# Router scores and choice per chunk of 128 tokens, and the shared expert's down products moved behind unit 9

## The chip, the core and the metric

The program runs on one core of a Trainium2 chip. The core has five engines with queues of their own: PE (TensorE, matrix products), DVE (VectorE), ACT (ScalarE), POOL (GpSimd) and SP (SyncE, which here does nothing but issue DMAs). Each queue is worked off in order; engines wait for each other through semaphores. The metric is the device time of one execution in microseconds (us).

## The reference

Two transformer blocks over 256 tokens of width 1024, one after the other. The first has a pooling mixer, an attention layer and two dense feed-forward layers. The second has a gated recurrent mixer and then a mixture of experts. Only the last part matters here, cut to this:

```
h   = rms_norm(x, g_pre_ffn) * (1 + sc2) + sh2            # 256 x 1024
s   = sigmoid(h @ w_router); sel = s + b_router           # 64 experts
# 8 groups of 8 experts; a group's score is the sum of its two best sel
# keep the 4 best groups, then the 8 best experts of those
w   = s[top8] / sum(s[top8]) * 2.5
y   = sum over the 8 experts e of w_e * swiglu(h, w_gu[e], w_down[e])
y  += swiglu(h, w_sh_gu, w_sh_down)                       # the shared expert
out = x + gt2 * rms_norm(y, g_post_ffn)
```

An expert has a 1024 x 512 gate-up matrix and a 256 x 1024 down matrix, 3 MB in float32. All 64 experts are read, 192 MB.

## The kernel before

All of it is one straight program; its author writes the order of each engine's instructions by hand. The 256 tokens are two chunks (c = 0, 1) of 128, one token per partition.

**Up to the router.** `post` ends the mixer: it forms the residual x (`resid`), the normed input of the experts (`second`, in the tile `yg`), turns it by PE transposes into `h2T` (`flip`, `copies`), and splits `yg` into a high and a low part in `h2` (`parts`: a cast on ACT, a subtraction on POOL). Then come the router's scores (one product for all 256 tokens, L1512, a sigmoid, two transposes back, L1518) and, in `route`, the choice on DVE for both chunks at once, which ends in the mask `M` of chosen experts, the weights `W`, and, through three small products with triangular and all-one matrices (L1557 to L1559), each token's rank within its expert (`slot1`).

**The shared expert's gate-up product** needs 16 float32 products of 128 x 128 by 512 (L1585). They are a generator, and `fill(n)` puts the next n of them into PE's queue, between the router's steps: `GU_AT` says how many at four places, and `route` issues what is left behind the rank products. Its down products (L1610, four groups, one for each chunk and half of the output) start the four PSUM accumulators `acc`, and stand inside unit 0: `first_fill` puts two groups where later units add the unit before them, and two follow with `self.down(1, 0)` and `self.down(1, 1)`.

**The units.** The 64 experts are worked off in 28 units, `UNITS = "FFFFSSMHMSMMHMSMMHMSMMMHSMMM"`: F and M hold two experts with room for 64 tokens each, S four with 32, H one with 128. For every second unit PE gathers the tokens of two units (L1792). Then each unit has a gate-up product `front` (L1809), the silu on ACT and its product on DVE (L1814), and `back`: transposes (L1824, L1829), the down product (L1841), and split results that the next unit adds into `acc` (L1853). `sides()` hides the placement of experts into units behind units 0 to 4; from unit 4 on the expert to load is read from its result, `plan`.

**The loads.** Expert weights come as tiles of 128 x 2048 floats (1 MB), three for each expert (two gate-up, one down), issued on SP's queue in the order of use (L1735) into 17 slots: 11 of the tag `ex` in the pool `ep`, and 6 in `ep2`, which opens when the dense weights are gone. A slot is taken again in the order in which its users end in the program. At the start `yg` holds one of the 11 slots, the shared expert's weights three (`wsh`, L1746), and seven take expert tiles. So 3 + 7 + 6 loads go ahead of the router, and the next ones wait in turn for `yg`, the two gate-up tiles of `wsh`, the six tiles of unit 0, the down tile of `wsh`, the tiles of unit 1, and so on. From the 25th expert tile on, a tile takes the slot of the tile 17 places before it. `self.loads(...)` only puts issues into SP's queue; when they start is decided by the slots.

One more transfer: the row `GP2`, 1024 gains spread over 128 partitions (512 KB, POOL's queue, L173), needed only at the end, is read behind unit 0's front.

Of the kernel before, what the change touches and what calls it, by code (L numbers as in the profile page):

```python
# [22 lines left out]
TAIL = 2  # L23
# [66 lines left out]
GU_AT = (4, 1, 1, 6)  # L90
# [58 lines left out]
class Kern:  # L149
# [936 lines left out]
    def mixer(self):  # L1086
# [320 lines left out]
    def post(self, ctx, ws_ctx):  # L1407
# [17 lines left out]
        lg = tmp[0:64, 128:384]  # L1425
# [13 lines left out]
        def resid(c, h, r, eng):  # L1439
            sl = hs[h]  # L1440
            V.scalar_tensor_tensor(x[:, c, sl], yg[:, c, sl], r, x[:, c, sl], op0=ALU.mult, op1=ALU.add)
            eng.tensor_tensor(yg[:, c, sl], x[:, c, sl], G2[:, sl], op=ALU.mult)

# [44 lines left out]
        resid(1, 0, r, nc.gpsimd)  # L1488
        resid(1, 1, r, nc.gpsimd)
# [4 lines left out]
        self.loads(3 + NEX - 4 + NEX2)  # L1494
        flip(0)
# [20 lines left out]
        self.pl = self.pst([128, 2, 64])  # L1516
        for c in range(2):
            nc.tensor.transpose(self.pl[:, c, :], lg[:, 128 * c:128 * c + 128], self.ident[0:64, 0:64])  # L1518
        self.dump("xl2", x)


    def route(self):

        nc, A = self.nc, self.A
        tmp = _Arena(self.small([128, 1024], "grow", 3))
        t3 = lambda tag, shape=(128, 2, 64): tmp.tile(list(shape))
        br, tri8, pl = self.br, self.tri8, self.pl
        self.fill(GU_AT[3])
        sel = t3("sel")
        nc.vector.tensor_tensor(sel, pl, br[:, None, :].to_broadcast([128, 2, 64]), op=ALU.add)  # L1530

        m8 = t3("m8", (128, 16, 8))
        sg = sel.rearrange("p c (g e) -> p (c g) e", e=8)
        for i in range(16):
            nc.vector.max(m8[:, i, :], sg[:, i, :])
        gs = t3("gs", (128, 2, 8))
        nc.vector.tensor_tensor(gs.rearrange("p c g -> p (c g)"), m8[:, :, 0], m8[:, :, 1], op=ALU.add)
        g8, gn = t3("g8", (128, 2, 8)), t3("gn", (128, 2, 8))
        for c in range(2):
            nc.vector.max(g8[:, c, :], gs[:, c, :])  # L1540
        nc.vector.memset(g8[:, :, 4:8], -3.0e38)
        for c in range(2):
            nc.vector.match_replace(gn[:, c, :], g8[:, c, :], gs[:, c, :], -3.0e38)
        nc.vector.tensor_tensor(gn, gn, gs, op=ALU.is_equal)
        nc.vector.copy_predicated(sg, gn.rearrange("p c g -> p (c g)")[:, :, None].to_broadcast([128, 16, 8]).bitcast(I32),
# [3 lines left out]
        for c in range(2):  # L1549
            nc.vector.max(top[:, c, :], sel[:, c, :])  # L1550
# [193 lines left out]
    def tiles(self):  # L1744
# [3 lines left out]
        for n in range(NUNIT):  # L1748
            yield from self.load_unit(n)
# [346 lines left out]
```

## Time and profile before

| | |
|---|---|
| three timed runs | 1332.06, 1332.54, 1334.05 us; median 1332.54 us |
| the profiled execution | 1334.75 us, of which the span from first to last instruction is 1332.9 us (1.85 us lie around it) |
| busy share of the span | PE 96%, PE weight loads 69%, DVE 48%, ACT 39%, POOL 17% |
| moved by DMA | 374.45 MB; the slices from 933 us to 1300 us show 405 to 421 GB/s each, the mean of the span is 281 GB/s |
| granted PE clock, mean | 0.988 of full speed |

The dense part fills the span up to about 830 us, the router lies between 830 and 853 us, and the 28 units follow up to 1323 us. An engine's busy time counts its instructions from start to end. A timeline's row gives the start, the length, the engine, the line of the kernel, the operation, what is written and read (a tile's name without its number), the shape and how many instructions were merged; in brackets stands how long the engine sat idle before it and what ended that. A float32 product counts as two PE instructions. The granted clock 1.00 is the level of 2.4 GHz, 0.50 that of 1.2 GHz.

### The profile page before, as it was taken

Reading aid. Unit: us, or ns where it says so; the run is one execution under the profiler, and the core shown is the slowest. Engines: PE = TensorE matmul, PEld = TensorE weight load, DVE = VectorE, ACT = ScalarE, POOL = GpSimd, SP = SyncE. Lnnn points to the kernel's source line nnn. Section 1 sums busy time; section 2 is a strip of 40 time slices with the busy share of each in tenths; the row PEclk is TensorE's granted clock in tenths of the full one; section 3 lists DMA queues with packets and bytes.
Section 4 is the critical chain, followed back from the end, with each engine's and each line's share of the span. In section 5 each row is a group of like instructions: output and inputs, shape, how many; then the busy total and the mean of one; then the engine's idle time right before and its main releaser. Section 6 shows DMA issues by size and latency. Waiting matters only on the chain. (4 is left out here: it accounts for less than half of the span.)

```text
span 1332.9 us, 20200 instructions
## 1 busy us (share of the span) xinstructions
PE 1274.2 (96%) x7812; PEld 922.1 (69%) x7812; DVE 646.2 (48%) x984; ACT 526.0 (39%) x883; POOL 228.3 (17%) x230
## 2 busy tenths in 40 slices
PE   7999999999999999989988899999998999999986
PEld 5889887988798998878887897544453443534532
DVE  5664555846657456576879557423222222222223
ACT  6534444557554456556645345311111111111112
POOL 1111112123033000125246442200000000000000
PEclk8999999999999999999999999999999999999998
DMA  8768678444485575646434478799999999999994
GB/s 301 252 231 280 248 270 316 155 164 159 130 326 189 189 249 194 221 151 242 143 104 136 152 274 342 273 372 378 405 420 420 419 420 419 420 419 420 421 420 192
DMA packets 72817, 374.45 MB, mean 281 GB/s; under 512 B 8932, under 2 KB 9364, under 8 KB 44304
## 3 DMA queue, kind: packets, MB, share of 16 engines
q1 hardware_dynamic: 68912, 361.25, 71.3%
q0 software_dynamic: 3664, 11.89, 2.8%
q8 instruction: 62, 1.02, 0.3%
q14 instruction: 35, 0.29, 0.1%
q10 hardware_dynamic: 144, 0.01, 0.0%
HBM read 371.99 MB, written 1.11 MB: 280 GB/s over the span
## 5 line engine op out<-in xcount | busy, mean ns | idle before, releaser
L137 DVE TENSOR_TENSOR wlo<-wland,whi 128x1024 fp32r<-128x1024 f32 x201 | 244.2, 1249 | 104.4 <-ACT whi L134 103.6
L258 PE MATMUL pw<-hT,whi 128*128 128x256 f32 x1856 | 250.6, 282 | 0.0
L134 ACT CAST whi<-wland 128x1024 fp32r<-128x1024 f32 x236 | 237.2, 1046 | 25.2 <-PE pa L267 12.7
L258 PEld LDWEIGHTS pw<-hT,whi 128*128 128x128 f32 x1856 | 232.9, 189 | 12.6 <-ACT whi L134 6.5
L1809 PE MATMUL pw<-ex,xg 128*64 128x512 f32 (+2 forms) x1024 | 208.5, 596 | 5.0 <-DMA ex<-ex 4.8
L1809 PEld LDWEIGHTS pw<-ex,xg 128*64 128x64 f32 (+2 forms) x1024 | 65.7, 130 | 133.3 <-issue 107.4
L258 PE MATMUL pw<-hT,wlo 128*128 128x256 f32 x928 | 128.2, 280 | 0.0
L1841 PE MATMUL pw<-ex,al 128*64 128x512 f32 (+2 forms) x512 | 113.2, 613 | 7.9 <-DMA ex<-ex 7.9
L258 PEld LDWEIGHTS pw<-hT,wlo 128*128 128x128 f32 x928 | 117.2, 189 | 0.2 <-POOL wlo L137 0.2
L137 POOL TENSOR_TENSOR wlo<-wland,whi 128x1024 fp32r<-128x1024 f32 x35 | 87.4, 2497 | 162.7 <-ACT whi L134 127.9
L267 PE MATMUL pa<-whi,hT 128*128 128x512 f32 x352 | 114.6, 401 | 0.0
L1814 DVE TENSOR_TENSOR a<-sil,pw 128x256 f32<-128x256 f32 x28 | 11.8, 421 | 190.5 <-ACT sil L1812 190.5
L1846 DVE SCALAR_TENSOR_TENSOR grow<-pw,sw,yh 128x512 fp32r<-128x512 f32 x56 | 42.1, 751 | 111.9 <-ACT yh L1845 111.0
L1812 ACT ACTIVATE sil<-pw 128x256 f32<-128x256 f32 x28 | 10.8, 385 | 209.0 <-PE pw L1809 209.0
L700 POOL TENSOR_TENSOR al<-a,ah 128x256 fp32r<-128x256 f32 x44 | 32.6, 742 | 326.9 <-ACT ah L699 326.9
L1841 PEld LDWEIGHTS pw<-ex,al 128*64 128x64 f32 (+2 forms) x512 | 31.9, 132 | 74.9 <-issue 49.9
L1845 ACT ACTIVATE yh<-pw,sw 128x512 fp32r<-128x512 f32 x56 | 38.5, 688 | 111.1 <-PE pw L1841 111.1
L694 ACT ACTIVATE sil<-pw 128x256 f32<-128x256 f32 x44 | 16.9, 384 | 164.7 <-PE pw L258 164.7
L1780 POOL TENSOR_TENSOR grow<-hx,Wp 128x256 f32<-128x256 f32 x24 | 14.7, 630 | 383.7 <-DVE hx L1778 383.7
L267 PEld LDWEIGHTS pa<-whi,hT 128*128 128x128 f32 x352 | 66.5, 189 | 16.1 <-DVE hT L248 0.4
L267 PE MATMUL pa<-wlo,hT 128*128 128x512 f32 x176 | 70.2, 399 | 5.0 <-DVE wlo L137 3.4
L267 PE MATMUL pa<-wlo,ah 128*128 128x512 f32 x176 | 69.8, 397 | 0.5 <-DVE wlo L137 0.5
(400 smaller groups left out, 1780.8 us busy)
## 6 DMA issues: line engine op xcount, KB each, us to landing
ex<-ex SPq DMA_DIRECT2D x192, 1024.0 KB
wland<-wd SPq DMA_DIRECT2D x236, 512.0 KB
ada<-ada SPq DMA_DIRECT2D x24, 1024.0 KB
row<-rows POOLq DMA_DIRECT2D x6, 512.0 KB, 4.9
ex<-exs SPq DMA_DIRECT2D x3, 1024.0 KB
bias<-bscr POOLq DMA_DIRECT2D x4, 512.0 KB, 4.8
x<-x SPq DMA_DIRECT2D x4, 256.0 KB
pw<-poolw SPq DMA_DIRECT2D x2, 512.0 KB
```

Source lines behind the costliest of these rows:

```text
L134: nc.scalar.copy(h, t)
L137: eng.tensor_tensor(l, t, h, op=ALU.subtract)
L258: self.nc.tensor.matmul(out, a[:, o:o + 128], b[:, k, :], start=(p == 0 and k == 0), stop=(p == 2 and k == nk - 1))
L267: self.nc.tensor.matmul(out, a[:, k, cs], b[:, lo:lo + n], start=(first and p == 0), stop=(last and p == 2))
L694: nc.scalar.activation(sil, ps[:, 0:256], AF.Silu)
L700: nc.gpsimd.tensor_tensor(al[:, 0, :], a, ah[:, 0, :], op=ALU.subtract)
L1780: nc.gpsimd.tensor_tensor(view(ow), view(oh), W[:, :, :, None].to_broadcast(shape), op=ALU.mult)
L1809: nc.tensor.matmul(gu[r * e:r * e + r, :], xg[:, k, o + r * e:o + r * e + r], w[k // 4][:, 512 * (k % 4):512 * (k % 4) + 512], start=(k == ...
L1814: nc.vector.tensor_tensor(act, sil, gu[:, 256:512], op=ALU.mult)
L1841: nc.tensor.matmul(y[r * e:r * e + r, :], aT[:, f, r * e:r * e + r], w[2][:, 1024 * f + 512 * nb:1024 * f + 512 * nb + 512], start=(f == 0 ...
L1845: nc.scalar.activation(yh[:, sl], y, AF.Copy, scale=sw)
L1846: nc.vector.scalar_tensor_tensor(yl[:, sl], y, sw, yh[:, sl], op0=ALU.mult, op1=ALU.subtract)
```

## The change

The scores are computed with the tokens on the partitions at once: per chunk eight products with 64 columns (`logits`), a sigmoid (`scores`), and the choice on DVE (`choose`, for one chunk). Chunk 0's choice is put ahead of chunk 1's scores in the program. All of `yg`'s gains for chunk 1 go to DVE (POOL before). Seven shared gate-up products now stand ahead of the rank products and nine behind (twelve and four before; the last number of `GU_AT` is not used any more). The shared expert's down products go behind unit 9 (`DOWN_AT`): unit 0 then starts the accumulators, the down weights are loaded behind unit 8's tiles into an ordinary slot, an eighth expert tile takes their old slot at the start, and the load of `GP2` stands behind the down products.

```diff
-GU_AT = (4, 1, 1, 6)
+GU_AT = (4, 1, 2, 2)
+DOWN_AT = 9
...
-                self.ex, self.nload, self.nex = {}, 0, 4
+                self.ex, self.nload, self.nex = {}, 0, 3
                 self.yg = self.tile8([128, 2, 1024])
-                self.wsh = [self.tile8([128, 2048]) for _ in range(3)]
+                self.wsh = [self.tile8([128, 2048]) for _ in range(2)]
...
+        acc = [first(1, 0)]
         r0 = self.rstd(sx[0], 1024)
-        acc = [first(1, nb) for nb in range(2)]
+        acc.append(first(1, 1))
...
-        resid(1, 0, r, nc.gpsimd)
-        resid(1, 1, r, nc.gpsimd)
+        for h in range(2):
+            sums(1, h, r)
+        for h in range(2):
+            gains(1, h, V)
...
+        def logits(c):
+            for k in range(8):
+                nc.tensor.matmul(pl[:, c, :], h2T[:, k, 128 * c:128 * c + 128], wrt[:, k, :], start=(k == 0), stop=(k == 7))
+
+        def scores(c):
+            nc.scalar.activation(lg[:, c, :], pl[:, c, :], AF.Sigmoid)
+
         flip(0)
         copies(0, nc.scalar.copy, nc.scalar.copy)
+        logits(0)
         sqx(1, 0)
         sqx(1, 1)
         r1 = self.rstd(sx[1], 1024)
         self.warm(AF.Sigmoid)
+        scores(0)
         self.shared = self.shared_products()
         self.fill(GU_AT[0])
         for h in range(2):
             second(1, h, r1)
         flip(1)
-        copies(1, nc.scalar.copy, V.tensor_copy)
+        copies(1, nc.scalar.copy, nc.scalar.copy)
+        choose = self.choices()
+        choose(0)
+        self.fill(GU_AT[1])
+        logits(1)
         parts(0)
+        scores(1)
+        self.warm(AF.Silu)
         parts(1)
-        self.fill(GU_AT[1])
-        pg = self.pst([64, 256])
-        for k in range(8):
-            nc.tensor.matmul(pg, wrt[:, k, :], h2T[:, k, :], start=(k == 0), stop=(k == 7))
-        nc.scalar.activation(lg, pg, AF.Sigmoid)
-        self.warm(AF.Silu)
+        choose(1)
         self.fill(GU_AT[2])
...
+        def go(c):
+            V.tensor_tensor(sel[:, c, :], lg[:, c, :], br, op=ALU.add)
+
+            sg = sel[:, c, :].rearrange("p (g e) -> p g e", e=8)
+            for i in range(8):
+                V.max(m8[:, c, i, :], sg[:, i, :])
+            V.tensor_tensor(gs[:, c, :], m8[:, c, :, 0], m8[:, c, :, 1], op=ALU.add)
...
+            V.copy_predicated(sg, gn[:, c, :, None].to_broadcast([128, 8, 8]).bitcast(I32),
+                              self.low[:, :, None].to_broadcast([128, 8, 8]))
...
+            V.tensor_tensor(M[:, c, :], rep[:, c, :], sel[:, c, :], op=ALU.not_equal)
...
         for i in range(3):
+            if i == 2:
+                for n in range(DOWN_AT):
+                    yield from self.load_unit(n)
+                self.wsh.append(self.tile_ex())
             self.nc.sync.dma_start(out=self.wsh[i], in_=self.A["exs"][:, 2048 * i:2048 * i + 2048])
             yield 1
-        for n in range(NUNIT):
+        for n in range(DOWN_AT, NUNIT):
             yield from self.load_unit(n)
...
-            if n == 0:
-                GP2 = self.row(self.rows, 7 * 1024, 1024)
-                pend = first_fill
...
             if n == 0:
-                self.down(1, 0)
                 next(side)
-                self.down(1, 1)
+            if n == DOWN_AT:
+                done += 1
+                for c in range(2):
+                    for nb in range(2):
+                        self.down(c, nb)
+                GP2 = self.row(self.rows, 7 * 1024, 1024)
```

PE's queue from the transposes of chunk 1 (`flip(1)`) to the first gather, before; L1585 are the shared gate-up products, L1557 to L1559 the rank products:

```order
L1462 MATMUL pt<-cst,ex 128x128 x8
L1585 MATMUL pw<-ex,h2T 128x512
L1512 MATMUL pt<-h2T,hx 64x256 x8
L1585 MATMUL pw<-ex,h2T 128x512
L1518 MATMUL pt<-cst,hx 128x64 x2
L1585 MATMUL pw<-ex,h2T 128x512 x6
L1557 MATMUL pt<-M,cst 128x64
L1558 MATMUL pt<-M,cst 128x64
L1559 MATMUL pt<-M,cst 128x64
L1585 MATMUL pw<-ex,h2T 128x512 x4
L1792 MATMUL pt<-hx,h_8186 128x256 x32
```

Six shared products stand between the scores (L1518) and the rank products, four behind them. The same place in the changed kernel; L1603 are the shared gate-up products now, L1510 the router's, L1585 to L1587 the rank products, L1815 the gather:

```order
L1470 MATMUL pt<-cst,ex 128x128 x8
L1603 MATMUL pw<-ex,h2T 128x512
L1510 MATMUL pa<-hx,h2T 128x64 x8
L1603 MATMUL pw<-ex,h2T 128x512 x2
L1585 MATMUL pt<-M,cst 128x64
L1586 MATMUL pt<-M,cst 128x64
L1587 MATMUL pt<-M,cst 128x64
L1603 MATMUL pw<-ex,h2T 128x512 x9
L1815 MATMUL pt<-hx,h_8186 128x256 x32
```

Two shared products are left between the scores and the rank products, and nine stand behind; the third rank product is the one that waits for chunk 1's mask.

PE's queue in unit 0 from the end of its front to unit 1, before (L1667, L1672 and L1674 belong to the placement):

```order
L1610 MATMUL pa<-ex,al 128x512 x2
L1824 MATMUL pt<-cst,a_8552 128x128 x2
L1829 MATMUL pt<-cst,grow 128x128 x2
L1610 MATMUL pa<-ex,al 128x512 x2
L1841 MATMUL pw<-ex,al 64x512 x8
L1672 MATMUL pt<-hx 128x60
L1674 MATMUL pt<-hx,cst 128x60
L1672 MATMUL pt<-hx 128x60
L1674 MATMUL pt<-hx,cst 128x60
L1610 MATMUL pa<-ex,al 128x512 x2
L1667 MATMUL pt<-cst,sc 64x128 x2
L1610 MATMUL pa<-ex,al 128x512 x2
```

The four groups of two down products (L1610) stand among unit 0's own steps. In the changed kernel:

```order
L1686 MATMUL pt<-cst,sc 64x128 x2
L1847 MATMUL pt<-cst,a_8568 128x128 x2
L1852 MATMUL pt<-cst,grow 128x128 x2
L1864 MATMUL pw<-ex,al 64x512 x8
L1691 MATMUL pt<-hx 128x60
L1693 MATMUL pt<-hx,cst 128x60
L1691 MATMUL pt<-hx 128x60
L1693 MATMUL pt<-hx,cst 128x60
L1686 MATMUL pt<-cst,sc 64x128 x2
```

The eight down products (L1610) are gone from here; between the front and the transposes of `a`, and between these and the down product of unit 0, PE has nothing else to do.

## Rows read from the trace of the kernel before

**Rows 1.** The page, part 1: busy us, share of the span, instructions.

```profile
PE 1274.2 (96%) x7812; PEld 922.1 (69%) x7812; DVE 646.2 (48%) x984; ACT 526.0 (39%) x883; POOL 228.3 (17%) x230
```

**Rows 2.** Stretches: length, busy PE, PEld, DVE, ACT, POOL, granted clock, DMA share, GB/s.

```profile
840.00:850.00 10.00, 10.00 (x35) 5.01 (x34) 5.13 (x39) 2.26 (x5) 3.48 (x3) 1.00 0.62 231
930.00:940.00 10.00, 10.00 (x84) 4.31 (x80) 1.31 (x4) 0.76 (x2) 0.00 (x0) 1.00 0.93 361
```

**Rows 3.** DMA queues, 1000 to 1300 us: packets, MB, share of 16 engines.

```profile
q1 hardware_dynamic: 17259, 125.71, 101.0%
```

**Rows 4.** Issues of line L1735 from 932.5 us on: count, lengths, first to last start.

```profile
L1735 SPq DMA_DIRECT2D ex<-ex x151: 332/333/456, 932.8 to 1295.3; - x151
```

**Rows 5.** Timeline of PE around the router.

```profile
836.68 1.29 PE L1462 MATMUL pt<-cst,ex 128*128 128x128 f32 x8 [0.57 <-DVE ex L1449]
...
838.77 3.67 PE L1512 MATMUL pt<-h2T,hx 128*64 128x256 f32 x16
...
848.94 0.33 PE L1557 MATMUL pt<-M,cst 128*128 128x64 f32 x2
...
849.55 3.65 PE L1585 MATMUL pw<-ex,h2T 128*128 128x512 f32 x8
```

**Rows 6.** Timeline of ACT around the router.

```profile
837.83 2.18 ACT L1453 CAST h<-ex 128x512 fp32r<-128x512 f32 x4
842.47 0.38 ACT L1513 ACTIVATE hx<-pt 64x256 f32<-64x256 f32 x1 [2.46 <-PE pt L1512]
842.87 1.28 ACT L183 ACT_TABLE_LOAD   x1
```

**Rows 7.** Timeline of DVE: first and last step to the mask, unit 0's product.

```profile
843.79 0.29 DVE L1530 TENSOR_TENSOR grow<-pt,hx 128x128 f32<-128x128 f32 x1 [5.09 <-PE pt L1518]
...
847.69 0.29 DVE L1554 TENSOR_TENSOR M<-grow 128x128 f32<-128x128 f32 x1
...
866.16 0.42 DVE L1814 TENSOR_TENSOR a<-sil,pw 128x256 f32<-128x256 f32 x1 [0.86 <-ACT sil L1812]
```

**Rows 8.** Timeline of POOL: the subtractions of `parts`.

```profile
838.53 4.96 POOL L1454 TENSOR_TENSOR h<-ex,h 128x512 fp32r<-128x512 f32 x4 [2.54 <-ACT h L1453]
```

**Rows 9.** Timeline of all engines from 585 to 588.5 us.

```profile
585.50 2.38 POOL L137 TENSOR_TENSOR wlo<-wland,whi 128x1024 fp32r<-128x1024 f32 x1 [2.38 <-ACT whi L134]
...
585.60 2.31 DVE L1055 SCALAR_TENSOR_TENSOR r<-ss,r 128x1 f32<-128x1 f32 x1
```

**Rows 10.** Stretches in which PE stands still, and the stretch behind each.

```profile
587.90:591.20 3.30, 0.00 (x0) 0.00 (x0) 2.81 (x7) 3.11 (x10) 0.00 (x0) 1.00 0.52 158
592.10:595.40 3.30, 2.68 (x9) 2.33 (x10) 2.72 (x7) 0.98 (x4) 2.61 (x1) 0.50 0.00 0
703.10:706.10 3.00, 0.00 (x0) 0.00 (x0) 3.00 (x4) 0.00 (x0) 2.64 (x2) 1.00 0.00 0
706.20:709.60 3.40, 3.40 (x19) 2.91 (x20) 3.40 (x3) 1.81 (x3) 3.32 (x4) 1.00 0.50 159
759.80:763.40 3.60, 0.00 (x0) 0.00 (x0) 3.57 (x3) 0.38 (x1) 2.95 (x2) 0.90 0.45 146
763.50:769.40 5.90, 5.90 (x28) 5.90 (x29) 4.86 (x4) 1.53 (x2) 2.38 (x1) 0.50 0.95 350
```

**Rows 11.** Timeline of PE in unit 0 and at the start of unit 1.

```profile
865.85 1.88 PE L1610 MATMUL pa<-ex,al 128*128 128x512 f32 x4
...
869.82 3.65 PE L1841 MATMUL pw<-ex,al 128*64 128x512 f32 x16
...
878.28 1.08 PE L1809 MATMUL pw<-ex,xg 128*64 128x512 f32 x4
```

**Rows 12.** DMA queues, 845 to 862 us: the row `GP2` alone on this queue.

```profile
q0 software_dynamic: 144, 0.52, 11.0%
```

**Rows 13.** Waits of PE's weight loads from 1026 us on: total, times, longest.

```profile
PEld pw L1841 <- DMA ex<-ex: 11.0, 6, 2.4
PEld pw L1809 <- DMA ex<-ex: 10.2, 10, 2.3
```

More of the change, by code (lines that the diff above doesn't have):

```diff
@@ L1514, in post @@
-        self.warm(AF.Silu)
+        choose(1)
         self.fill(GU_AT[2])
-        self.pl = self.pst([128, 2, 64])
-        for c in range(2):
-            nc.tensor.transpose(self.pl[:, c, :], lg[:, 128 * c:128 * c + 128], self.ident[0:64, 0:64])
         self.dump("xl2", x)
-    def route(self):
[L1524 to L1545, printed above, removed]
-                                  self.low[:, :, None].to_broadcast([128, 16, 8]))
-        top, rep = t3("top", (128, 2, 8)), t3("rep")
-        for c in range(2):
-            nc.vector.max(top[:, c, :], sel[:, c, :])
-        for c in range(2):
-            nc.vector.match_replace(rep[:, c, :], top[:, c, :], sel[:, c, :], -3.0e38)
-        M = self.small([128, 2, 64], "M", 1)
-        nc.vector.tensor_tensor(M, rep, sel, op=ALU.not_equal)
@@ new lines, in choices @@
+    def choices(self):
+        nc = self.nc
+        V = nc.vector
+        tmp = _Arena(self.small([128, 1024], "grow", 3))
+        t3 = lambda shape=(128, 2, 64): tmp.tile(list(shape))
+        br, tri8, lg = self.br, self.tri8, self.lg
+        sel, m8, gs, g8, gn = t3(), t3((128, 2, 8, 8)), t3((128, 2, 8)), t3((128, 2, 8)), t3((128, 2, 8))
+        top, rep, wsum = t3((128, 2, 8)), t3(), t3((128, 2))
+        self.slot1 = t3()
+        self.M = M = self.small([128, 2, 64], "M", 1)
+        ws = self.small([128, 2, 2, 64], "sc", 1)
+        self.W, self.slot = W, _ = ws[:, 0], ws[:, 1]
+        V.memset(g8[:, :, 4:8], -3.0e38)
+        def go(c):
[4 more added lines that the diff above has]
+            V.tensor_tensor(gs[:, c, :], m8[:, c, :, 0], m8[:, c, :, 1], op=ALU.add)
+            V.max(top[:, c, :], gs[:, c, :])
+            V.tensor_copy(g8[:, c, 0:4], top[:, c, 0:4])
+            V.match_replace(gn[:, c, :], g8[:, c, :], gs[:, c, :], -3.0e38)
+            V.tensor_tensor(gn[:, c, :], gn[:, c, :], gs[:, c, :], op=ALU.is_equal)
+            V.copy_predicated(sg, gn[:, c, :, None].to_broadcast([128, 8, 8]).bitcast(I32),
+                              self.low[:, :, None].to_broadcast([128, 8, 8]))
+            V.max(top[:, c, :], sel[:, c, :])
+            V.match_replace(rep[:, c, :], top[:, c, :], sel[:, c, :], -3.0e38)
+            V.tensor_tensor(M[:, c, :], rep[:, c, :], sel[:, c, :], op=ALU.not_equal)
+            V.tensor_tensor(W[:, c, :], lg[:, c, :], M[:, c, :], op=ALU.mult)
+            V.reduce_sum(wsum[:, c:c + 1], W[:, c, :], axis=AX.X)
+            V.reciprocal(wsum[:, c:c + 1], wsum[:, c:c + 1])
+            V.tensor_scalar(W[:, c, :], W[:, c, :], wsum[:, c:c + 1], 2.5, op0=ALU.mult, op1=ALU.mult)
+        return go
@@ L1847, in back, with scatter @@
             return oT, yh, yl
-        def scatter(oT, *y):
+        def scatter(oT, *y, start=False):
             def go(c, nb, parts=(0, 1)):
@@ L1852, in go @@
                 for i in parts:
-                    nc.tensor.matmul(self.acc[c][nb], oT[:, c, :], y[i][:, sl], start=False, stop=(i == 1),
+                    nc.tensor.matmul(self.acc[c][nb], oT[:, c, :], y[i][:, sl], start=(start and i == 0), stop=(i == 1),
                                      skip_group_check=True)
@@ L1878, in sides @@
             yield from self.overflow()
-        def first_fill(c, nb):
-            if c == nb:
-                self.down(0, nb)
         side = sides()
-        oh, done = onehot(two(0, self.slot1), self.iota1), 3
+        oh, done = onehot(two(0, self.slot1), self.iota1), 2
         nc.vector.tensor_scalar(self.slot, self.slot1, -1.0, None, op0=ALU.add)
@@ L1901, in experts @@
                 oh = onehot(two(n + 1))
-            pend = scatter(*back(ws, act, grp[1], n % 2, pend))
+            pend = scatter(*(back(ws, act, grp[1], n % 2, pend) if n else back(ws, act, grp[1], 0)), start=(n == 0))
             next(side, None)
             if n == 0:
-                self.down(1, 0)
                 next(side)
-                self.down(1, 1)
+            if n == DOWN_AT:
[4 more added lines that the diff above has]
+                GP2 = self.row(self.rows, 7 * 1024, 1024)
             self.loads(done + NEX + NEX2 + 12)
```

32 lines of the change are left out of this document (15 added, 17 removed).

## The prediction

> **What bounds the kernel now.** The page's first part names PE: busy for 96% of the span [rows 1]. But PE is busy by its modelled ends, so the stretches come next. From 840 to 940 us PE is busy 10.00 us of each 10 while the DMA engines move 231 to 361 GB/s [rows 2]; behind that, from 1000 to 1300 us, the DMA engines are full: 101.0%, 125.71 MB in 300 us [rows 3], so 2.50 us for a tile of 1.0486 MB. The issues on SP tell where the one turns into the other: 151 of the 192 expert tiles are issued from 932.8 us on [rows 4], and 151 times 2.50 is 378 us, which ends at 1310. In this stretch PE is the one that waits: behind unit 9 alone (1026 us) its weight loads wait 21.2 us for `ex` [rows 13]. So two limits follow each other. Up to 932.8 PE sets the pace: the tile issued there (the 42nd) takes the slot of the 25th, which unit 4 gives back in the middle of its front. From there bytes count. The end moves by what PE gains or loses up to unit 4, plus 2.50 us for each MB that is added behind it.
>
> **The change part by part.** The sum is made against the profiled execution (1334.75 us), which lies 2.2 us above the median of the runs shown, 1332.54; its differences are put on the median.
>
> *PE up to the rank products.* These started at 848.94 [rows 5]. A shared product takes 0.91 us (3.65 for eight instructions, four products). Five of them leave this place: 4.5 us earlier. The router's 16 products of 64 columns take 0.20 each if they run at the pace of the three rank products of the same shape (0.61 us from 848.94 to 849.55), so 3.3 us in place of 3.67 and of two transposes (0.3): 0.7 us earlier. The wait of 0.57 us ahead of chunk 1's transposes is covered by `logits(0)`. PE is there at about 843.2.
>
> *When chunk 1's mask is ready.* Two products stand between its scores and the rank products, so the scores end at about 841.4 on PE; with the sigmoid (0.38) [rows 6] and the ways between engines DVE starts at about 842.1. For both chunks DVE took 843.79 to 847.98 [rows 7]. One chunk halves the 16 maxima and the doubled rows, but not the chain of dependent steps: I estimate 2.9 us. That is 845.0, if nothing is in the way.
>
> *What is in the way.* POOL's subtractions of `parts` ran ahead of the choice before, four of 1.24 us from 838.53 to 843.49 [rows 8]; the choice began behind them. Now those of chunk 0 follow their casts (0.55 us each) at about 840.5 to 843.0. The casts of chunk 1 stand behind the second sigmoid and a table load of 1.28 us [rows 6], so their subtractions run from about 844.4 to 846.9. Both pairs lie on the choice of chunk 1. And a DVE step that reads two tiles in SBUF stands still while such a POOL instruction runs: a step on a single element a lane took 2.31 us, to 587.91, beside a subtraction that ended at 587.88 [rows 9]. In the choice the addition of the bias (its scores came from PSUM before, and come from SBUF now), the addition of the maxima, the comparisons and the predicated copy are of that kind. The Trainium skill says it as a rule ("SBUF — State Buffer", Who interferes with whom): the port pair that DVE shares with GpSimd is an exclusive lock, which a DVE instruction with two SBUF inputs contends for, and the later one blocks until the first is done. Rows 9 agree. By the rule the mask comes late, as in what follows; without it the time would be that of the first rival. In the order of the steps the bias waits for the last subtraction of chunk 0 (842.1 to about 843.1), and the steps from the comparison of the groups on wait once or twice for those of chunk 1, until 845.7 and 846.9. The mask is then ready at 847.4 to 848.2. I take 847.8. Bounds: 845.0 and 848.2.
>
> *From there to unit 0.* The rank products start at 847.8, 1.1 us earlier than before, but nine shared products follow instead of four: 4.5 us more. The gather starts **3.4 us later** (0.6 if nothing blocks, 3.8 at most).
>
> *The clock.* PE then stands still from 843.5 to 847.8, but for one rank product of chunk 0. It did so three times in these rows: 3.3 us at 587.9 and 3.6 at 759.8 were followed by a granted clock of 0.50, the lower level of 1.2 GHz, for at least 3.3 and 5.9 us; 3.0 us at 703.1 was followed by 1.00 [rows 10]. Shared products and gather at the lower level lose half of such a stretch, 1.7 to 3.0 us. I take **2.3 us**; bounds 0 and 3.0.
>
> *Unit 0.* The four groups of down products (1.88 us each) go: 7.6 us [rows 11]. They also covered waits. `a` is ready 0.75 us behind the last transposes ahead of it (866.16 and 0.42 [rows 7], against PE free at 865.85), and its transposes, the copy and their ways cost about 0.95 more before the down product, which began at 869.82. So 1.7 us of waiting stay, and unit 1 starts **5.9 us earlier** against unit 0 (bounds 5.0, if the placement's copies are late too, and 6.4). Up to unit 4 nothing else changes on PE.
>
> *The slots.* One expert tile more is loaded at the start, and the shared down tile fills no slot until unit 9. In both kernels the 42nd tile waits for the 25th, with 151 tiles to go; the changed kernel has the down tile to load besides: **2.5 us**. The tile of `yg`'s slot is issued some 3 us later, since POOL ends `parts` later; the DMA engines have time for it, at 0.62 of their share in that stretch [rows 2].
>
> *`GP2`.* Its 0.52 MB were moved while the DMA engines had room, and are now moved while they are full. 11.0% of 17 us is 1.9 us of all engines [rows 12], by its bytes alone 1.25. I take **1.9**.
>
> *The down products behind unit 9* cost PE 7.5 us where it waits for tiles. Its 21.2 us of waits behind that place [rows 13] are the cover: a unit that starts later waits less for its tiles. No DMA waits for the late PE: at unit 9's end PE has used all that has landed, so nearly all slots are empty. Without the cover it would be 7.5 us. The gains on DVE instead of POOL, the earlier square and the memset cost nothing: the path there ends in chunk 0's transposes first, then in `fill`.
>
> *The sum:* +3.4 +2.3 −5.9 +2.5 +1.9 = +4.2 us; 1338.95 against 1334.75, so **1336.7 us** by the median.
>
> **The rivals.**
> *1. Not slower: DVE isn't blocked.* If the subtractions fall between the steps, the mask is ready at 845.0, PE waits 1.7 us and keeps its clock: 0.6 − 5.9 + 4.4 = −0.9, **1331.6**. It decides when the mask is there before about 846. For it speaks that most steps are short and only some read two tiles, against it rows 9.
> *2. Blocked, but the clock stays at 1.00:* 3.4 − 5.9 + 4.4 = +1.9, **1334.4**. For it speaks 703.1 in rows 10, and that a rank product falls into the wait; against it the other two.
> *3. Bytes don't count:* if the tail has room for the down tile and `GP2`, which a share of 101% [rows 3] speaks against, then with rival 1 0.6 − 5.9 = −5.3, **1327.2**.
> *4. The down products aren't covered* behind unit 9: up to 7.5 us more, **1344**. Against it rows 13.
>
> **How the numbers follow.** The forecast has a chance of 0.53, rival 1 0.22, rival 2 0.15, rival 3 0.07, rival 4 0.03. A difference of 0.2% (2.7 us) is about what a measurement of this kernel tells from none. Faster by more: rival 3 and the far end of rival 1, 0.12. Within: most of rivals 1 and 2 and the mild end of the forecast (a lower clock of 1.7 us, `GP2` at 1.25), 0.39. Slower: the rest, 0.49. The range reaches from rival 1 with the larger gain in unit 0 (6.4) to the forecast with a mask at 848.2 and 3.0 us for the clock: 1331.0 to 1338.2; I leave half a us at both ends, 1330.5 to 1338.7.
>
> **What would show it.** In the new profile: PE idle for some 4 us ahead of the third rank product (L1587), released by DVE `M`; steps of the choice of over 1 us beside POOL's L1462; a granted clock of 0.50 behind it; unit 1's front about 6.5 us behind the end of unit 0's, where it was 12.4 (865.85 to 878.28 [rows 11]); 151 expert tiles and one of `exs` from the middle of unit 4 on, the first of them between 927 and 934 us; `GP2` near unit 9; no wait of the DMA queue on units 10 to 14. I am wrong if the choice isn't on PE's way, if the tile issued at the turn waits for something else than unit 4, or if bytes behind it don't move the end.

## The result and the profile after

The changed kernel took 1342.11 us (median of eight runs, 1336.16 to 1344.66), the kernel before 1334.24 (eight runs, the three of the table among them). The ratio is 1.0055, 95% interval 1.0041 to 1.0070: **7.3 us slower** by the ratio, 7.9 by the medians. The direction was forecast, the size was not; 1342.1 lies above the range. The profiled execution took 1339.36 us (span 1337.6), among the faster of the eight, so the kernel was profiled twice more below (1344.61 and 1342.19 us).

PE's timeline of the changed kernel, from the transposes of chunk 0 (`flip(0)`) to the gather, answers to [rows 5]:

```profile
828.49 0.63 PE L1470 MATMUL pt<-cst,ex 128*128 128x128 f32 x4 [1.30 <-DVE ex L1457]
829.75 0.63 PE L1470 MATMUL pt<-cst,ex 128*128 128x128 f32 x4 [0.63 <-DVE ss L199]
830.58 2.00 PE L1510 MATMUL pa<-hx,h2T 128*128 128x64 f32 x16 [0.20 <-ACT h2T L1475]
832.42 5.35 PE L1603 MATMUL pw<-ex,h2T 128*128 128x512 f32 x8
...
842.84 0.33 PE L1585 MATMUL pt<-M,cst 128*128 128x64 f32 x2
843.01 0.39 PE L1586 MATMUL pt<-M,cst 128*128 128x64 f32 x2
847.26 0.69 PE L1587 MATMUL pt<-M,cst 128*128 128x64 f32 x2 [3.87 <-DVE M L1573]
847.74 10.53 PE L1603 MATMUL pw<-ex,h2T 128*128 128x512 f32 x18
857.70 0.68 PE L1815 MATMUL pt<-hx,h 128*128 128x256 f32 x1
```

The wait of 3.87 us ahead of the third rank product is the one forecast. But two groups are slow: eight instructions on shared products took 5.35 us at 832.42 where 3.65 was usual, and the nine products behind the wait 10.53 us. The stretches of the same kernel show why; the first number behind POOL is the granted clock:

```profile
830.00:840.00 10.00, 9.80 (x45) 6.03 (x43) 8.23 (x35) 6.12 (x15) 0.09 (x1) 0.83 1.02 425
840.00:850.00 10.00, 6.13 (x25) 3.90 (x24) 7.71 (x28) 3.28 (x7) 5.87 (x6) 0.80 0.42 147
850.00:860.00 10.00, 10.00 (x32) 5.19 (x31) 0.84 (x2) 1.16 (x3) 0.24 (x1) 0.85 0.44 126
```

Before, 840 to 850 was at 1.00 [rows 2]. Here the clock fell to 0.50 (1.2 GHz) twice: at 832.4 for 3.4 us, before PE had come to the rank products, and at 846.1 for 6.8 us. Only the second was forecast.

DVE's timeline of the choice of chunk 1, which answers to [rows 7], and under it POOL's subtractions:

```profile
841.52 0.95 DVE L1558 TENSOR_TENSOR grow<-hx 128x64 f32<-128x64 f32 x1 [2.32 <-ACT hx L1513]
842.51 0.65 DVE L1562 MAX8 grow<-grow 128x8 f32<-128x8 f32 x8
...
843.60 1.27 DVE L1565 COPY grow<-grow 128x4 f32<-128x4 f32 x1
...
844.99 0.15 DVE L1566 MATCH_REPLACE8 grow<-grow 128x8 f32<-128x8 f32 x1
845.17 0.92 DVE L1567 TENSOR_TENSOR grow<-grow 128x8 f32<-128x8 f32 x1
...
846.98 0.22 DVE L1573 TENSOR_TENSOR M<-grow 128x64 f32<-128x64 f32 x1
```

```profile
839.91 2.49 POOL L1462 TENSOR_TENSOR h<-ex,h 128x512 fp32r<-128x512 f32 x2 [13.54 <-ACT h L1461]
843.59 2.48 POOL L1462 TENSOR_TENSOR h<-ex,h 128x512 fp32r<-128x512 f32 x2 [1.19 <-ACT h L1461]
```

The three long steps end at 842.47, 844.87 and 846.09; POOL's pairs end at 842.40 and 846.07, and half of the second pair at about 844.83. So each long step ends behind a subtraction. From 841.52 to the mask are 5.68 us.

PE's timeline behind unit 0's front, against [rows 11]: the shared down products are gone, and the waits for `a` and `al` are 0.62 and 0.24 us.

```profile
870.64 0.41 PE L1686 MATMUL pt<-cst,sc 128*64 128x128 f32 x2
871.67 0.44 PE L1847 MATMUL pt<-cst,a 128*128 128x128 f32 x2 [0.62 <-DVE a L1837]
...
872.58 3.65 PE L1864 MATMUL pw<-ex,al 128*64 128x512 f32 x16 [0.24 <-ACT al L1849]
...
877.53 0.65 PE L1832 MATMUL pw<-ex,xg 128*64 128x512 f32 x2
```

Last, the stretch behind unit 9. First the waits of the DMA queue on SP from 1000 to 1045 us (what it waited for, us in total, times, the longest), then the down products on PE, then two stretches:

```profile
SPq L1754 <- DMA ex<-ex: 18.2, 9, 4.1
SPq L1754 <- PE pa L1629: 15.7, 1, 15.7
```

```profile
1026.67 7.13 PE L1629 MATMUL pa<-ex,grow 128*128 128x512 f32 x16
```

```profile
1020.00:1030.00 10.00, 8.82 (x47) 3.20 (x46) 2.27 (x5) 1.75 (x3) 1.06 (x2) 1.00 1.01 419
1030.00:1040.00 10.00, 10.00 (x53) 6.24 (x53) 1.38 (x2) 1.17 (x2) 0.58 (x1) 1.00 0.89 318
```

An issue waited 15.7 us for the last shared down product (`pa`, 1033.8 us). Behind it the DMA engines, full everywhere else in this part, show a share of 0.89. The kernel before has no wait above 0.3 us there but for its own transfers, and a share of 1.01 or more:

```profile
SPq L1735 <- DMA ex<-ex: 31.0, 18, 2.1
SPq L1735 <- PE pw L1809: 0.3, 1, 0.3
```

The turn itself came where forecast: the 42nd expert tile was issued at 932.0 us.

### The profile page after: what moved, and what is told of

It is laid out like the page before. It is cut to its first block, busy times and chain, and to the rows that moved or that the text cites. A ratio compares the mean times of both kernels' runs of the same rounds, so it can differ in the third digit from the quotient of the medians.

```text
span 1337.6 us, 20231 instructions
## 1 busy us (share of the span) xinstructions
PE 1276.0 (95%) x7826; PEld 924.9 (69%) x7826; DVE 650.7 (49%) x996; ACT 526.7 (39%) x885; POOL 225.1 (17%) x228
## 5 line engine op out<-in xcount | busy, mean ns | idle before, releaser
L1864 PE MATMUL pw<-ex,al 128*64 128x512 f32 (+2 forms) x512 | 109.4, 598 | 6.8 <-DMA ex<-ex 6.6
```

The lines of the kernel that those rows point to most:

```text
L1864: nc.tensor.matmul(y[r * e:r * e + r, :], aT[:, f, r * e:r * e + r], w[2][:, 1024 * f + 512 * nb:1024 * f + 512 * nb + 512], start=(f == 0 ...
```

## The experiments

Three stretches of PE's timeline describe each profile: from `flip(0)` to the gather (with the part of it at a clock of 0.50), from unit 0's front to unit 1's, and from there to PE's end. The ratio is to the kernel before, run beside it.

| kernel | median us | ratio (95%) | flip(0) to gather (at 0.50) | unit 0 to 1 | unit 1 to end |
|---|---|---|---|---|---|
| before | 1334.24 | | 22.32 (0) | 21.24 | 444.34 |
| changed | 1342.11 | 1.0055 (1.0041–1.0070) | 29.21 (10.2) | 15.44 | 449.80 |
| r1_after, one run | 1344.61 | | 30.86 (13.7) | 15.44 | 449.76 |
| r2_after, one run | 1342.19 | | 30.27 (13.7) | 15.44 | 449.78 |
| e1_router | 1341.96 | 1.0063 (1.0050–1.0076) | 26.43 (3.4) | 21.24 | 444.31 |
| e2_down | 1332.58 | 0.9995 (0.9984–1.0006) | 22.60 (3.4) | 15.45 | 450.04 |
| e3_fill | 1336.01 | 1.0012 (1.0001–1.0022) | 24.57 (6.8) | 15.45 | 449.74 |
| e4_parts | 1335.11 | 1.0007 (0.9993–1.0022) | 25.48 (6.8) | 15.45 | 449.75 |
| e5_both | 1334.23 | 1.0003 (0.9991–1.0015) | 23.51 (6.8) | 15.45 | 450.08 |
| e10_busy | 1337.88 | 1.0032 (1.0020–1.0045) | 28.07 (6.8) | 15.44 | 449.85 |
| e11_order | 1331.78 | 0.9989 (0.9978–1.0001) | 20.96 (0) | 15.45 | 449.74 |
| e6_nodown | 1328.73 | 0.9963 (0.9950–0.9976) | 23.03 (3.4) | 15.45 | 445.81 |
| e7_gp2 | 1332.71 | 0.9986 (0.9977–0.9995) | 22.55 (3.4) | 15.45 | 448.96 |
| e8_down2 | 1340.96 | 1.0048 (1.0035–1.0060) | 22.62 (3.4) | 15.44 | 456.77 |
| e9_ahead | 1332.11 | 0.9985 (0.9976–0.9993) | 22.61 (3.4) | 15.45 | 448.24 |
| e12_best | 1332.50 | 0.9981 (0.9968–0.9993) | 20.96 (0) | 15.44 | 448.04 |

The last two columns repeat within 0.4 us for kernels that don't differ there; so they price a part better than the runs do.

**1. Which half.** The theory: the router's half loses ahead of the gather, the down products' half gives back less than it takes. The first rival: the two transfers in the full stretch make the loss. e1_router has the changes in `post`, `choices` and `route` and `GU_AT = (4, 1, 2, 2)`, and the rest as before; e2_down has the other half, with `GU_AT = (4, 1, 1, 6)`.

> Only the router's half of the change: scores and choice per chunk, seven shared products ahead of the rank products and nine behind; the down products, their tile and GP2 stay in unit 0 as before. My theory: the loss is all made here, in the wait for chunk 1's mask and at the lower clock behind it, and is kept up to the turn where the DMA engines become full. The profile of the changed kernel has the gather 6.9 us later against flip(0) than before (forecast 5.7), so 6 to 7 us slower than before, with no gain in unit 0 to set against it. Rival: the loss is made behind unit 4 by the two transfers put there, and what PE loses ahead of the turn is taken back where it waits for tiles; then within 1.5 us of before.

> Only the other half: the shared expert's down products, their tile and GP2 behind unit 9, the router as before. My theory: unit 1 starts 5.9 us earlier, and one tile and GP2 in the stretch of full DMA engines give 4.4 us back (the changed kernel's profile shows 5.5 from the 42nd tile to the end): 0.4 to 1.5 us faster than before, which is within 0.2%. Rival: what the down products cost behind unit 9 isn't covered, up to 7.5 us; then 1.5 to 6 us slower than before. Other rival: the bytes are hidden anyway, then 5 to 6 us faster.

The halves add up: 0.63% slower, and 0.05% faster, which the runs can't tell from none; both together 0.55% slower. The loss is the router's. It is even a little more than expected of e1_router: 7.5 us by the medians, 8.4 by the ratio. Its profile, of the fastest of its five runs (1338.97 us), shows 4.1 us of it (26.43 against 22.32 to the gather): it has no fall of the clock ahead of the rank products, and one of 3.4 us behind the wait. e2_down lies where the theory put it: 5.8 us won in unit 0, 5.7 lost behind it.

**2. The wait and what is in the way.** e3_fill puts work into PE's wait; e4_parts takes POOL off the choice.

```diff
-GU_AT = (4, 1, 2, 2)
+GU_AT = (4, 1, 6, 2)
```

> The changed kernel with one number changed: six shared products in place of two between chunk 1's scores and the rank products, so five instead of nine behind. My theory: the mask comes when it came (about 847), the four products fill PE's wait of 3.87 us, and the clock has no reason to fall behind it. The gather starts 3.7 us earlier for the wait and about 2.0 for the clock: 5 to 6 us faster than the changed kernel, so about 1 us slower than before, up to 1 faster. Rival: the clock falls anyway, because of the drop at 832 (64-column products behind waits); then 3 to 4 us faster than the changed kernel. Rival: what is saved ahead of the turn isn't kept; then no difference from the changed kernel.

```diff
             for sl in hs:
                 nc.scalar.copy(h2[:, 0, c, sl], yg[:, c, sl])
-                nc.gpsimd.tensor_tensor(h2[:, 1, c, sl], yg[:, c, sl], h2[:, 0, c, sl], op=ALU.subtract)
...
+        def lows(c):
+            for sl in hs:
+                V.tensor_tensor(h2[:, 1, c, sl], yg[:, c, sl], h2[:, 0, c, sl], op=ALU.subtract)
...
         choose(1)
+        for c in range(2):
+            lows(c)
```

> The changed kernel with the four subtractions of the low parts on DVE behind the choice of chunk 1, none on POOL. My theory: the choice of chunk 1 is then not held up: its steps with two inputs take 0.17 to 0.25 us like chunk 0's, where they took 0.95, 1.27 and 0.92; the mask is ready at about 844.4 (847.0 in the changed kernel), PE waits about 1.3 us instead of 3.87 and keeps its clock: 3 to 5 us faster than the changed kernel. Rival: the long steps are long for another reason (waits for ACT's or DVE's own results); then the mask still comes at about 847 and the time is that of the changed kernel.

Both mechanisms held. e3_fill was 6.1 us faster than the changed kernel by the medians and 5.7 by the ratios, as expected; e4_parts 7.0 and 6.4, which is more than the 3 to 5 expected. The choice of chunk 1 in e4_parts, DVE's timeline, and PE's third rank product:

```profile
842.23 0.23 DVE L1563 TENSOR_TENSOR grow<-hx 128x64 f32<-128x64 f32 x1 [3.97 <-ACT hx L1516]
842.49 0.64 DVE L1567 MAX8 grow<-grow 128x8 f32<-128x8 f32 x8
...
843.58 0.17 DVE L1570 COPY grow<-grow 128x4 f32<-128x4 f32 x1
...
843.86 0.15 DVE L1571 MATCH_REPLACE8 grow<-grow 128x8 f32<-128x8 f32 x1
844.05 0.17 DVE L1572 TENSOR_TENSOR grow<-grow 128x8 f32<-128x8 f32 x1
...
845.10 0.23 DVE L1578 TENSOR_TENSOR M<-grow 128x64 f32<-128x64 f32 x1
```

```profile
845.38 0.43 PE L1592 MATMUL pt<-M,cst 128*128 128x64 f32 x2 [1.28 <-DVE M L1578]
```

The three steps take 0.23, 0.17 and 0.17 us in place of 0.95, 1.27 and 0.92, and scores to mask takes 3.10 us in place of 5.68. A step with one input was not held up: MATCH_REPLACE8 takes 0.15 us in both, and in the changed kernel it ran beside a subtraction. (The eight maxima, 0.64 and 0.65, don't tell: from 842.51 to 843.16 they ran while POOL paused.) PE waits 1.28 us. The Trainium skill ("SBUF — State Buffer", Who interferes with whom) says that DVE steps with two SBUF inputs, and copies in a two-port mode, contend with a GpSimd instruction that reads SBUF, and that the one that comes later blocks fully. The trace agrees: 2.58 us of blocking, on an addition and a comparison with two inputs and on a copy; whether the copy ran in such a mode, no view shows.

With PE's wait gone or short, a clock of 0.50 was left in both, 6.8 us of it between 830 and 840, ahead of the rank products. e5_both has both edits, with `GU_AT = (4, 1, 4, 2)`.

> The changed kernel with both mendings: the subtractions of the low parts on DVE behind the choice, and four shared products (not two) between chunk 1's scores and the rank products. Alone, each of them brought the time from 1342 to 1335 or 1336, and in both runs the clock was at 0.50 for 6.8 us from about 831 on, ahead of the rank products. My theory: the mask is ready at about 845 and PE comes there at about 845.5, so PE has no wait left, only the work of the router; the gather starts about 1.5 us earlier than with the subtractions alone: 1332 to 1334, 0.5 to 2 us faster than before. Rival: the wait was all that could be saved by either, and the clock's fall at 831 takes the rest; then 1335, as with the subtractions alone.

It came out between: 1334.2, the wait gone (23.51 us to the gather, 2 less than with the subtractions alone), the clock's fall still there.

**3. The clock.** e10_busy leaves the wait's length and makes PE busy in it.

```diff
+        spare = self.pst([128, 512])
+        for i in range(4):
+            nc.tensor.matmul(spare, self.h2T[:, i, 0:128], self.wsh[0][:, 512 * i:512 * i + 512], start=True, stop=True)
         nc.tensor.matmul(pp[:, 1, :], self.upper, M[:, 1, :], start=False, stop=True)
```

> The changed kernel with four products of the shared expert's shape, whose result nobody reads, put into PE's wait between the second and the third rank product. They take 3.65 us at full clock where PE stood still for 3.87, so nothing starts earlier by it; only PE is busy. My theory: the clock's fall behind the wait (0.50 from 846.1 to 852.9 in the changed kernel's profile) goes, and with it 2.3 us as I put it in the prediction, up to 4: 1338 to 1340, against 1342. Rival: the clock falls for what was ahead (64-column products, the waits around flip) or falls elsewhere instead; then 1341 to 1343.

1337.88 us, just below the 1338 to 1340 expected: 4.2 us less than the changed kernel by the medians and 3.1 by the ratios, with no product of the kernel starting earlier by it. PE's rank product and the nine products behind, and the two stretches:

```profile
848.10 0.43 PE L1590 MATMUL pt<-M,cst 128*128 128x64 f32 x2 [0.39 <-DVE M L1573]
848.37 7.94 PE L1606 MATMUL pw<-ex,h2T 128*128 128x512 f32 x18
```

```profile
840.00:850.00 10.00, 9.61 (x39) 5.42 (x38) 7.14 (x28) 4.29 (x9) 5.14 (x5) 1.00 0.28 91
850.00:860.00 10.00, 10.00 (x47) 6.51 (x45) 2.03 (x5) 1.56 (x3) 1.08 (x2) 1.00 0.69 238
```

7.94 us for what took 10.53. From the third rank product to the gather it is 7.65 us here and 10.44 in the changed kernel, so the fall behind the wait costs 2.8.

> The changed kernel once more, for a second profile. Its timed runs went from 1336.2 to 1344.7 us with mean granted clocks of 0.987 down to 0.980; the profiled one had 0.985 and 1339.4. My theory: the clock is at 0.50 at one or two of four places (at 832, behind the wait at 846, at 1013, at 1275) for 3.4 or 6.8 us in different runs, and that is the difference between runs. Rival: the place is the same each time and something else differs, such as the DMA engines' rate.

> The same once more, a third profile of the changed kernel; expected as in the second: a clock of 0.50 behind the wait at 846 in each of the three, and at 832 in some.

Both have the fall behind the wait, for 6.8 us, and one ahead of the rank products, also for 6.8. r1_after on PE, and its stretch:

```profile
834.21 3.58 PE L1510 MATMUL pa<-hx,h2T 128*128 128x64 f32 x16 [0.20 <-ACT h2T L1475]
837.59 5.44 PE L1603 MATMUL pw<-ex,h2T 128*128 128x512 f32 x8
```

```profile
830.00:840.00 10.00, 7.87 (x31) 5.67 (x30) 8.96 (x29) 5.96 (x16) 0.00 (x0) 0.72 1.01 419
```

The 16 products of 64 columns took 3.58 us, where the first profile has 2.00. From `flip(0)` to the first rank product it is 14.35, 15.98 and 15.62 us in the three profiles, and 12.66 in e1_router, where the clock stayed at 1.00 up to there: this fall costs 1.7, 3.3 and 3.0 us. Of the 5.3 us between the first profile and r1_after, 1.7 lie here; the other 3.6 lie ahead of `flip(0)`, where the clock is at 0.50 for 30.7 us in r1_after and for 20.5 in the first profile. So each theory had a part of it: the place is the same, the length is not, and the dense part has its own falls.

What made it fall was open. Six profiles with the old router have 0 to 3.4 us of it, six of eight with the new one have 6.8. e11_order is e5_both with one more edit:

```diff
         copies(0, nc.scalar.copy, nc.scalar.copy)
-        logits(0)
...
-        scores(0)
         self.shared = self.shared_products()
         self.fill(GU_AT[0])
+        logits(0)
+        scores(0)
```

> The kernel with both mendings of the router (1334.2 us), and besides chunk 0's scores put behind the first four shared products instead of ahead of them, so that 512-column products follow the waits at flip(0), as they did before the change. My theory: the 16 products of 64 columns directly behind the waits lengthen the stretch at 0.50 (6.8 us in six of the eight profiles of kernels with the new router, 3.4 in five of the six with the old one); then it is 3.4 us or none, the gather starts 22.5 us behind flip(0) (23.5 in the kernel that it is made from) and the time is 1332 to 1333. Rival: the waits alone make the clock fall, and the order changes nothing: 6.8 us at 0.50 and 1334 to 1335.

```profile
830.44 3.70 PE L1608 MATMUL pw<-ex,h2T 128*128 128x512 f32 x8 [0.20 <-ACT h2T L1478]
833.98 1.89 PE L1513 MATMUL pa<-hx,h2T 128*128 128x64 f32 x16
...
849.31 0.92 PE L1820 MATMUL pt<-hx,h 128*128 128x256 f32 x3
```

```profile
828.00:838.00 10.00, 8.81 (x48) 6.00 (x48) 8.07 (x29) 6.35 (x15) 0.00 (x0) 1.00 1.02 424
838.00:848.00 10.00, 9.85 (x38) 5.41 (x37) 9.17 (x43) 3.48 (x7) 0.47 (x1) 1.00 0.36 132
```

With the same waits at `flip(0)` (1.30, 0.63 and 0.20 us) the clock stays at 1.00 in this profile and in that of e12_best. 20.96 us to the gather are 1.4 less than before the change, where the clock held too, and 2.5 less than in e5_both, where it fell for 6.8 us. The time went to 1331.8.

But that the order kept the clock isn't shown. Near 762 us, ahead of all that the change touches on PE, there is an earlier fall. It lasts 3.4 us in some executions and 6.8 in others, for one and the same program too: 6.8 in the first profile of the changed kernel, 3.4 in r1_after and r2_after. Sorted by it, the sixteen profiles read:

| fall near 762 us | products behind the waits of `flip(0)` | profiles | us at 0.50 there |
|---|---|---|---|
| 3.4 us | 512 columns | e2_down, e6_nodown, e7_gp2, e8_down2, e9_ahead | 3.4 in each |
| 3.4 us | 64 columns | r1_after, r2_after, e3_fill, e4_parts, e5_both, e10_busy | 6.8 in each |
| 6.8 us | 512 columns | before, e11_order, e12_best | 0 in each |
| 6.8 us | 64 columns | changed (first profile), e1_router | 3.4 and 0 |

e6_nodown, with 512 columns, on PE and in its stretch, and under them the stretch of e1_router, with 64:

```profile
830.17 5.40 PE L1586 MATMUL pw<-ex,h2T 128*128 128x512 f32 x8 [0.20 <-ACT h2T L1468]
```

```profile
828.00:838.00 10.00, 9.09 (x30) 4.59 (x31) 6.46 (x12) 6.63 (x16) 3.74 (x3) 0.83 1.02 423
```

```profile
830.00:840.00 10.00, 8.60 (x46) 5.74 (x46) 9.20 (x34) 6.03 (x15) 0.00 (x0) 1.00 1.02 423
```

In fifteen profiles of sixteen, all but the changed kernel's first, whether the clock falls at `flip(0)` goes with the fall near 762 us, whatever the order; e11_order and e12_best were profiled in executions of the kind in which it held in e1_router too. How long it falls goes with the order, where the fall near 762 us took 3.4 us: 3.4 us with wide products and 6.8 with narrow ones, also where it falls at the same distance behind the start of `flip(0)` (1.2 to 1.3 us in e2_down and e5_both, 2.2 in e6_nodown and r1_after). No profile shows the third edit in an execution of the other kind. Of e11_order's twelve runs six lie between 1330.2 and 1330.9 us, the profiled one among them, and six between 1332.6 and 1335.3, and the interval of its ratio overlaps that of e5_both.

**4. The stretch of the full DMA engines.** The next four start from e2_down. e6_nodown leaves out the down tile and its products, e7_gp2 the transfer of `GP2`, e8_down2 issues the products twice:

```diff
                 for c in range(2):
                     for nb in range(2):
                         self.down(c, nb)
+                        self.down(c, nb)
```

> Made from the kernel with the down half alone (1332.58 us): the shared expert's down tile isn't loaded and its eight down products are left out, so the output lacks the shared expert; GP2 stays. It prices the tile. My theory: the bytes count, 2.50 us for the tile, and the products cost nothing: 1330, 2 to 3 us faster than the kernel it is made from. Rival: the tile is hidden; then 1332.6. Other rival: the products count too, up to 7.5 us; then 1323 to 1328.

> Made from the kernel with the down half alone (1332.58 us): GP2 is set to ones in SBUF instead of being loaded, so the gains of the last norm are left out. It prices the transfer of 0.52 MB. By my sum 1.9 us faster than the kernel it is made from (1330.7), by its bytes alone 1.25 (1331.3); rival: it is hidden, no difference. The spread of the runs is near these sizes; the time from the 42nd expert tile to the end in the profile is read beside it.

> Made from the kernel with the down half alone (1332.58 us): each of the four groups of shared down products behind unit 9 is issued twice (the shared expert's part of the output is doubled). It doubles the cost that I took to be covered. My theory: PE waits for tiles behind unit 9 anyway (21.2 us of weight loads waiting for ex before the change), so 7.5 us more of products lie in these waits: no difference, within 1.5 us. Rival: not covered, 4 to 7.5 us slower (1336.5 to 1340).

e6_nodown was 4.2 us faster than e2_down from unit 1 to the end, where the tile alone should give 2.5; e7_gp2 1.1. (The runs can't tell e7_gp2 from e2_down: 1332.71 against 1332.58 by the medians, 1.2 us faster by the ratios.) And e8_down2 went against my theory: 6.7 us more. Its waits on SP and its stretch:

```profile
SPq L1737 <- PE pa L1612: 22.5, 1, 22.5
```

```profile
1030.00:1040.00 10.00, 10.00 (x34) 5.22 (x33) 0.00 (x0) 0.38 (x1) 0.58 (x1) 1.00 0.24 80
```

The down tile holds its slot until its last product. SP issues in order, so the tile that takes this slot keeps back eight more whose slots are free, and the DMA engines run dry: when the wait ends, nine issues follow from 1038.7 to 1044.7 us, where one in 2.5 us is usual. e9_ahead moves the block of `if n == DOWN_AT:` (products and `GP2`) ahead of unit 9's `front`, where PE waits for unit 9's tiles (PE is busy for 7.11 us from 1000 to 1010 in e2_down, and for 10.00 in e9_ahead).

> Made from the kernel with the down half alone (1332.58 us): the shared down products and the load of GP2 stand ahead of unit 9's front instead of behind its back. In the kernels with the products behind, SP's queue waits 15.6 us for the down tile's slot (released by the last product on acc) with eight more tiles behind it, and the DMA engines, full before, drop to a share of 0.88 and 0.95 in the two stretches of 10 us there, some 1.7 us lost; with the products doubled it was 22.5 us of waiting, a share of 0.24 and 7 us of time. My theory now: the products ahead of the front lie in PE's wait for unit 9's tiles, the slot is given back before SP comes to it, the hole is gone: 1.5 to 2 us faster than the kernel it is made from, about 1330.8, 0.25% faster than before. Rival, the one of my prediction: the products are covered where they are; then no difference.

The waits for `pa` shrink to 0.3 us, and the DMA engines stay full:

```profile
SPq L1737 <- DMA ex<-ex: 31.4, 17, 3.2
...
SPq L1737 <- PE pa L1612: 0.3, 1, 0.3
```

```profile
1030.00:1040.00 10.00, 10.00 (x48) 4.08 (x46) 2.15 (x5) 2.13 (x4) 0.00 (x0) 1.00 1.01 417
```

The last column of the table gives the prices. The slot: 450.04 − 448.24 = 1.8 us. The tile: 448.24 − 445.81 = 2.4. `GP2`: 450.04 − 448.96 = 1.1, or by 445.81 − 444.34, which has `GP2` alone on top, 1.5. By the medians e9_ahead gained less than expected, 0.5 us, by the ratios 1.3; the cause, the wait for the slot, is gone all the same.

**5. All mended.** e12_best is e11_order with the edit of e9_ahead.

> The kernel with the three mendings of the router, and the shared down products ahead of unit 9's front instead of behind its back, which gave 2.0 us in the profiles and 1.3 in the runs when done alone. My theory: that gain adds to what the order brings, 1330.5 to 1331.5 us, 0.2 to 0.3% faster than before, and no slower than the kernel with the old router and the products ahead of the front (1332.1). Rival: the new router's fall of the clock stays; then 1332.5 to 1333.

1332.50 us, ratio 0.9981: 0.19% faster than before, by the interval 0.07 to 0.32%, and 1.4 us to the gather kept. From e9_ahead (0.9985) the runs can't tell it. The expected 1330.5 to 1331.5 us were missed by 1 us, and the time is the rival's; its profile, of the fastest of its twelve runs (1329.06 us), has no fall at `flip(0)`, and the seven runs from 1332.2 to 1334.6 us have no profile.

## Why the prediction was right in kind and wrong in size

Terms in us, measured by the stretches of the table:

| term of the sum | predicted | measured |
|---|---|---|
| gather later, at full clock | +3.4 | +2.4 |
| the clock behind the wait | +2.3 | +2.8 |
| the clock ahead of the rank products | not in the sum | +2.7 (1.7, 3.3, 3.0) |
| unit 0 | −5.9 | −5.8 |
| the down tile | +2.5 | +2.4 |
| `GP2` | +1.9 | +1.2 (1.1 to 1.5) |
| the down products behind unit 9 | 0 | +1.8 |
| sum | +4.2 | +7.5 |

(Gather at full clock: 29.21 − 1.69 − 2.79 − 22.32. `GP2` in the sum: what the tile and the slot leave of 449.80 − 444.34.) These two are remainders, so the sum is that of the first profile, 6.6, with the clock's mean of three profiles put in. The runs say 7.3.

**The blocked mask and PE's wait** were right: 3.87 us of waiting, steps of about 1 us beside POOL, and e4_parts shows the cause by taking it away. Rival 1 fell with this. Clock aside, the gather came 1.0 us sooner than I had it: the mask was a little earlier, and the nine products take 7.65 us to the gather.

**The clock** was the first step that failed. I put 2.3 us on the wait ahead of the rank product and looked for no other place. The step "PE is there at about 843.2" costed the router's 16 products at full pace directly behind the waits of `flip(0)`, which the kernel before has too, with wide products behind them:

```profile
830.32 0.63 PE L1462 MATMUL pt<-cst,ex 128*128 128x128 f32 x4 [1.37 <-DVE ex L1449]
...
832.41 3.70 PE L1585 MATMUL pw<-ex,h2T 128*128 128x512 f32 x8 [0.20 <-ACT h2T L1467]
```

There the clock fell in the changed kernel's three profiles, and cost 2.7 us in the mean. The place isn't free with wide products either: the five profiles of the old router with a fall there need 0.2 to 0.7 us more to the gather than the kernel before (22.55 to 23.03 against 22.32), so up to 0.7 of the 2.7 isn't the change's. Where the clock held, the step was right: 12.66 us from `flip(0)` to the first rank product in e1_router, 12.9 in the prediction (843.2 − 830.32). Rival 2 fell with the changed kernel's own profile, and e10_busy, in which PE is busy and the fall behind the wait is gone, shows what it cost.

**The down products behind unit 9** were the second. "No DMA waits for the late PE: at unit 9's end PE has used all that has landed, so nearly all slots are empty" speaks of the slots, of which eight stood free when the wait ended, and says nothing of the queue. I gave SP's order no thought, though it was in the text of the kernel: the tile 17 places behind the down tile stands first, and waits. I had looked for waits of the queue on units 10 to 14; the wait stood on the shared products themselves, 15.7 us. 7.1 us of products cost 1.8, the next 7.1 cost 6.7 (e8_down2). Rival 4 had the right place and sign, with PE's waits as the wrong carrier.

**The bytes** counted, as forecast: 2.4 us for the tile. `GP2` was near its bytes (1.25), not its share on the queue (1.9). Rival 3 fell with e6_nodown and e7_gp2.

**The base.** Of the 5.4 us between 1336.7 and 1342.1, 3.3 are these terms, and 1.7 come from the median of three runs, 1332.54, on which the sum was put; with eight it was 1334.24. The rest is within what single runs differ by. Two slips of the prediction's sums change nothing here: four groups of 1.88 us are 7.5 us and not 7.6, and the far end of the range adds up to 1337.8 and not 1338.2 (3.8 + 3.0 − 5.9 + 4.4 on 1332.54).

What stays open: what makes the fall near 762 us last 3.4 us in one execution and 6.8 in another, with which the fall at `flip(0)` comes and goes; and whether the order of e11_order shortens that fall in an execution that has one, as the old router's does.

## What to carry to other kernels

Narrow products put directly behind waits can cost more than their own time: where the clock fell there, it stayed at 0.50 for 6.8 us with narrow products and 3.4 with wide ones, so wide ones are worth trying in that place. One profile of each kernel doesn't show what an edit does to the clock; compare executions that agree in the falls ahead of the edit. A tile that is held long keeps back all that stand behind its slot in an in-order queue, so use a late, extra tile while its engine waits for tiles anyway, not behind that. And a choice of small DVE steps wants no GpSimd work on SBUF beside it: 2.6 us of blocking came from work that could run later.

## What the runs showed of the hardware

- The granted clock fell at a place where PE had never been idle for more than 1.30 us at a time (waits of 1.30, 0.63 and 0.20 us with transposes between, then 64-column products), and in five profiles also with 512-column products in their place. At idle times of PE of 3.0 to 3.7 us, before the change, it had fallen at 592.0 and 762.7 us and stayed at 703.1 [rows 10], and it had fallen at 694.4, behind 3.53 us, a place that the prediction left out; in r2_after it fell behind the idle time that answers to 703.1 too (3.04 us), for 6.8 us.
- Falls of one execution went together: where the one near 762 us lasted 3.4 us, the clock fell again at `flip(0)` in eleven profiles of eleven, where it lasted 6.8 us, in one of five.
- The three profiles of one program show 3.4, 6.8 and 6.8 us at 0.50 in the same place. One kernel's times spread over 8.5 us, 1336.2 to 1344.7, with mean granted clocks of 0.987 to 0.980.
- A copy of four elements a lane took 1.27 us beside a GpSimd subtraction and 0.17 without.
